# Two tiles for the block inverses, rotated queries and keys used later, and one staging buffer for raw weights, in a hybrid attention and RWKV-7 layer

## The chip, the cores and the metric

The kernel runs on one core of a Trainium2 chip, as a single launch for a whole decoder layer. The metric is the device time of one execution in microseconds, the median of several executions. Five engines work side by side, each through its own list of instructions in order: TensorE (PE, with its weight loads shown apart as PEld), VectorE (DVE), ScalarE (ACT), GpSimd (POOL) and SyncE (SP), which here does nothing but issue transfers. ACT and POOL issue transfers as well.

## The reference

One layer over 16 meta tokens and 2048 tokens of width 1024: RMSNorm, one input projection into 4640 columns, two parallel mixers, a gated merge, a residual, a SwiGLU feed-forward block and a final RMSNorm.

```python
u = rms_norm(h, norm_mix_g[layer])
proj = u @ w_in[layer] + b_in[layer]
...
q = partial_rope(q, pos)
k = partial_rope(k, pos)
y_attn = sliding_window_sink_attention(q, k, v, attn_sinks[layer])
y_rwkv = rwkv7_time_mix(p_rwkv, rwkv_mix[layer], ...)
merged = (gates[..., :D_MODEL] * (y_attn @ w_br_attn[layer])
          + gates[..., D_MODEL:] * (y_rwkv @ w_br_rwkv[layer]))
h = h + merged @ w_o[layer]
f = rms_norm(h, norm_ffn_g[layer])
h = h + (jax.nn.silu(f @ w_ffn_gate[layer]) * (f @ w_ffn_up[layer])) @ w_ffn_down[layer]
return rms_norm(h, norm_final_g)[:, N_META:]
```

The attention is a window of 128 with eight query heads, two key heads, global meta keys and a sink per head. The RWKV-7 mixer is a delta-rule recurrence with a state of 64 by 64 for each of eight heads.

## The kernel before

**Dense work.** The 2048 tokens are cut into four blocks of 512. `phase_a(b)` norms block b and makes the input projection, 37 chunks of 128 columns (one of them partly repeats). `phase_c(b)` makes the two branch products and the merge (8 chunks of `w_br`, 8 half chunks of `w_o`), then the feed-forward part (22 chunks of `w_gate`, 22 of `w_up`, 22 half chunks of `w_down`). Phase a runs for all four blocks, then phase c for all four.

**Weights.** Each product is made from three products of numbers with shortened mantissas: a weight is split into a high part (ACT copies it into a shorter type) and a low part (DVE subtracts the high part from the raw value). `chunk` does that. A weight tile `w` holds both parts of one chunk; there are three of them (tag `wsp`). The first time that a chunk is used, which is in phase a of block 0 for `w_in` and in phase c of block 0 for all the others, `chunk` takes it in two halves of 512 columns: SP loads the half into a raw tile `wraw` of 256 KB, ACT makes the high part, DVE the low part, and then POOL writes the finished pair (1 MB) to `parts_d` in HBM. For blocks 1 to 3 the finished pair is loaded whole from `parts_d`, and no raw tile is used. So 37 chunks go through the raw tiles in phase a(0) and 82 in phase c(0), with 24 products of 512 columns (a few more in phase a) on each.

**Mixers.** `attn(ti)` (tiles of 128 tokens) and `rwkv(i, j)` (256 tokens, one pair of heads) are Python generators. Each `yield` is a place where dense products are put between two of their steps. TensorE's order is fixed in exactly this program order (class `InOrder`); the order of the other engines comes from a scheduler. The dense loops yield an estimated time for each few products; for every 4 of these units each mixer in progress moves one step, the kinds in turn (`tick`). One attention tile is in progress at a time, and a new one starts when the one before it is through. Before phase c(b) starts, all mixers of blocks up to b are run to their end.

**Attention tile.** SP loads the queries `q`, a copy with swapped rows `qr`, the keys `kl` and `kr` and the values `vl`. After a `yield`, POOL rotates the queries (three instructions, L945 to L947) and the keys (`roped`, L894 to L896), ACT and DVE split the keys into `kw` (`set_keys`) and half of the queries into `qs` (`parts(0)`). Two more `yield`s later TensorE makes the scores `psS` from `qs` and `kw`. The second half of the queries is split by `parts(1)` between the two groups of heads.

**Inverses.** In each `rwkv` unit POOL solves small triangular systems (31 pairs of a product and a sum on `pr` and `xv`), writes the result to HBM (`xt_d`), and reads it back in four transfers into the diagonal blocks of `td` (L804). DVE transposes parts of `td`, TensorE and ACT fill its other corner, and the four chained steps of the unit (`ch`) read `td` as an operand up to the last of them. There is one `td` for all units; of `vd`, a like tile for the values, there are two, taken in turn.

Of the kernel before, what the change touches and what calls it, by code (L numbers as in the profile page):

```python
# [19 lines left out]
F32 = mybir.dt.float32  # L20
# [7 lines left out]
P = 128  # L28
# [50 lines left out]
def layer(ctx, tc, x, meta, w_in, w_br, w_o, w_gate, w_up, w_down, w2a, a2, g2, vecs, sinks, gfin,  # L79
# [23 lines left out]
    def late(r):  # L103

        tc.keep_in_program_order(r)
        return r
# [3 lines left out]
    cp = pool("const")  # L110
    dp = pool("dram", space=DRAM)
    dn = pool("dense")
# [5 lines left out]
    def f32(ap):  # L118
        return ap.bitcast(F32)
# [90 lines left out]
    def chunk(src, name, key, pin=False):  # L210


        w = dn.tile([P, 2, D], F32R, tag="wsp", bufs=3, name=f"w_{name}")
        if key in parts_d:
            with tc.high_priority():
                S.dma_start(f32(w.rearrange("p q c -> p (q c)")), parts_d[key])
            return w[:, 0], w[:, 1]
        for hf in range(2):
            c = slice(hf * 512, (hf + 1) * 512)
            with tc.high_priority():  # L220
                raw = dn.tile([P, 512], F32, tag="wraw", bufs=2, name=f"wr_{name}_{hf}")
                r = S.dma_start(raw, src[:, c])
                if name == "in_0_%d" % ORDER[0]:
                    late(r)
            made = HA.activation(w[:, 0, c], raw, AF.Copy), HV.tensor_sub(w[:, 1, c], raw, f32(w[:, 0, c]))
            if pin:
                late(made[0]), late(made[1])
        parts_d[key] = dp.tile([P, 2 * D], F32, name=f"wd_{name}")
        HG.dma_start(parts_d[key], f32(w.rearrange("p q c -> p (q c)")))
        return w[:, 0], w[:, 1]  # L230
# [133 lines left out]
    def phase_a(b):  # L364
        u = nxt[0] or rows_of(b)
        nxt[0] = None
        rest = None
        ws = []
        mid = lambda ci: lambda: ws.append(chunk(w_in[ci], f"in_{b}_{ci}", ("in", ci), True))
        for n_, ci in enumerate(ORDER):  # L370
            w = ws.pop(0) if ws else chunk(w_in[ci], f"in_{b}_{ci}", ("in", ci))
            if ci == ORDER[20] and b < NB - 1:
                nxt[0] = rows_of(b + 1)
            if ci == ORDER[-1] and b == NB - 1:
                nxt[0] = Ys(0)
            yield from in_chunk(b, ci, u, w, nxt[0] if ci == ORDER[-1] else None, mid(ORDER[n_ + 1]) if b == 0 and n_ < 2 else None)
            if rest:
                rest()
                rest = None
            if b == 0 and ci == ORDER[0]:  # L380
                load_rest()
                meta_norm()
            if b == 0 and ci in META_CH:
                rest = meta_chunk(ci, w)
            else:
                emitted[b].add(ci)

    def add_to_h(h, ms, src, name, key, last=None):


        ws = {}

        def part(t, hf):
            if hf not in ws:
                ws[hf] = chunk(src[hf], f"{name}_{hf}", key + (hf,))
            w = ws[hf]
            c = slice(hf * 512, (hf + 1) * 512)
            ps = psd.tile([P, 512], F32, tag="pd", name=f"ph_{name}_{t}_{hf}")
            q = slice(t * P, (t + 1) * P)
            for k in range(2):  # L400
                v = slice(k * 512, (k + 1) * 512)
                mm3(ps, ms[k][:, 0, q], ms[k][:, 1, q], w[0][:, v], w[1][:, v], k == 0, k == 1)
                yield 0.65
            HV.scalar_tensor_tensor(h[:, t, c], ps, 0.5, h[:, t, c], op0=ALU.mult, op1=ALU.add)

        if last is None:
            for hf in range(2):
                for t in range(4):
                    yield from part(t, hf)
        else:  # L410
            for t in range(4):
                for hf in range(2):
                    yield from part(t, hf)
                    last(t, hf)
# [134 lines left out]

    bkd = cp.tile([P, 2, 4, P], F32, name="bkd")  # L550
    vds = [cp.tile([P, 4, P], F32, name=f"vd{q}") for q in range(2)]
    td = cp.tile([P, 4, P], F32, name="td")
    rd = cp.tile([P, P], F32, name="rd")
    ud = cp.tile([P, P], F32, name="ud")
    for t in (bkd, *vds, td, rd):
        G.memset(t, 0.0)
    gmask = cst[:, _CC["gstrict"][0]:_CC["gincl"][1]]

# [58 lines left out]
    def rwkv(i, j):  # L617
# [3 lines left out]
        m = i is None  # L621
        uid = 4 * NU if m else 4 * i + j
# [152 lines left out]
        yield  # L775

        bt = mx.tile([P, 2, n, P], F32, tag="bt", bufs=2, name=f"bt_{nm}")
        vd = vds[(uid + m) % 2]
        for x in range(2):
            pb = psg.tile([P, 512], F32, tag="pg", name=f"pb_{nm}_{x}")  # L780
            for c in range(n):
# [98 lines left out]
    def set_keys(k, cols):  # L880
        for g in range(2):
            gb = slice(64 * g, 64 * g + 64)
            for d in (gb, slice(64 - 64 * g, 128 - 64 * g)):
                A.activation(kw[d, g, 0, cols], k[gb], AF.Copy)
                V.tensor_sub(kw[d, g, 1, cols], k[gb], f32(kw[gb, g, 0, cols]))
# [6 lines left out]
    def roped(o, src, rot, cs, w, name):  # L892

        G.tensor_mul(src, src, cs[:, 0])  # L894
        G.tensor_mul(rot, rot, cs[:, 1])
        G.tensor_add(o, src, rot)  # L896
# [28 lines left out]
    def attn(ti):  # L925
# [7 lines left out]
        q = mx.tile([P, 4, P], F32, tag="q", bufs=1, name=f"q_{ti}")  # L933
# [6 lines left out]
        load_rot(kr, 4, 1, c0, P)  # L940
        vt = mx.tile([P, P], F32, tag="vl", bufs=1, name=f"vl_{ti}")
        S.dma_start(vt, proj_d[5][:, c0:c0 + P])
        yield
        b4 = lambda k: cs[:, k].unsqueeze(1).to_broadcast([P, 4, P])
        G.tensor_mul(q, q, b4(0))  # L945
        G.tensor_mul(qr, qr, b4(1))
        G.tensor_add(q, q, qr)  # L947
        roped(kl[:, 0], kl[:, 0], kr[:, 0], cs, P, ti)
        set_keys(kl[:, 0], own)

        def parts(g):
# [75 lines left out]
    def tick():  # L1027

        turn[0] = (turn[0] + 1) % TURNS
        rs = [u for u in units if u[2] == "r"]  # L1030
        for u in list(units):
            if turn[0] != (0 if u[2] == "a" else 1 if len(rs) > 1 and u is rs[0] else 2):
                continue
            u[1] += 1
            if next(u[0], 0) == 0:
                units.remove(u)
        if todo_r and turn[0] == 2:
            i, j = todo_r[0]
            b = (i or 0) // 2
            young = min((u[1] for u in units if u[2] == "r"), default=LAG)  # L1040
            if young >= LAG - 3 and i not in asked and set(range(6, 9)) <= emitted[b]:
                asked.add(i)
                start("l", lora(i), b)
            if young >= LAG and i in loras and set(
                    range(9, 21) if i is None else range(PAIR0 + 3 * j, PAIR0 + 3 * j + 3)) <= emitted[b]:
                todo_r.pop(0)
                start("r", rwkv(i, j), b)
        if todo_a and turn[0] == 0 and not any(u[2] == "a" for u in units):
            ti = todo_a[0]
            b = (ti or 0) // 4  # L1050
            if set(range(6)) <= emitted[b]:
                todo_a.pop(0)
                start("a", attn_meta() if ti is None else attn(ti), b)
# [135 lines left out]
```

## Time and profile before

| what | us |
| --- | --- |
| median of 3 runs | 3381.07 (3380.14 to 3383.0) |
| profiled execution, own time | 3377.94 |
| its span, first to last instruction | 3376.0 |
| TensorE busy in it | 3256.3 (96%) |
| VectorE, ScalarE, GpSimd busy | 1542.1, 1163.2, 1156.1 |
| mean granted TensorE clock | 0.987 of full speed |

The profile is one execution of the kernel. Busy time of TensorE is modelled for pipelined products, so a busy TensorE isn't one at its peak. Idle time of another engine costs nothing unless TensorE waits for it in the end. Releasers of waits are inferred from semaphore events; a wait for several things is put down to the last of them. L202 is the line of a helper through which much of the dense work is recorded at high priority, so such work is told apart by its tiles.

### The profile page before, as it was taken

The page shows a single profiled execution, that of the slowest core. Times are in us where ns is not written, and L with a number is a line of the kernel's source. Part 1 is how long each engine was busy: PE and PEld are TensorE (multiplying, and loading weights), DVE is VectorE, ACT ScalarE, POOL GpSimd, SP SyncE. Part 2 cuts the span into 40 slices and gives each one's busy share as a digit, 9 for nine tenths or more (in the row PEclk, how much of TensorE's full clock was granted, in tenths as well). Part 3 has the DMA queues.
Part 4 walks back from the last instruction along what each step waited for, and adds up shares of the span by engine and source line. Part 5 has one row for each costly group of instructions (what it writes and reads, how often), then busy time and mean ns, then how long its engine had stood idle before and what let it go on. Part 6 is the DMA issues. An engine that isn't in the chain of part 4 may idle for free.

```text
span 3376.0 us, 47237 instructions
## 1 busy us (share of the span) xinstructions
PE 3256.3 (96%) x16909; PEld 2681.2 (79%) x16909; DVE 1542.1 (46%) x3622; ACT 1163.2 (34%) x2863; POOL 1156.1 (34%) x2771
## 2 busy tenths in 40 slices
PE   7899999999999998999999999999999999999998
PEld 6777887787888777887787788887888888778887
DVE  3343233232332585666666644445654443542233
ACT  4354344443443455445443422233242221220001
POOL 1124434334344454554453433444333341000000
PEclk9999999999999999999999999999999999999999
DMA  7777666676666776666668555556755555855555
GB/s 262 273 261 241 209 226 211 190 227 197 223 210 215 242 260 206 234 235 234 231 237 280 176 170 174 179 181 201 263 171 177 171 177 176 288 179 191 196 191 181
DMA packets 229448, 721.46 MB, mean 214 GB/s; under 512 B 36333, under 2 KB 90989, under 8 KB 168286
## 3 DMA queue, kind: packets, MB, share of 16 engines
q1 hardware_dynamic: 158126, 516.15, 47.1%
q0 software_dynamic: 38736, 154.99, 12.9%
q10 hardware_dynamic: 32352, 47.31, 3.8%
q8 instruction: 133, 2.18, 0.3%
q14 instruction: 101, 0.83, 0.1%
HBM read 533.46 MB, written 184.82 MB: 213 GB/s over the span
## 4 chain that ended last, share of the span: by engine, by line
PE 60%; DMA 6%; DVE 3%; POOL 3%; ACT 2%; issue 2%; SPq 0%; POOLq 0%; DVEq 0%; ACTq 0%
PE pg L93 14%; PE pu L93 12%; PE ph_d L93 11%; PE pi L93 6%; PE pb L93 4%; PE ch L93 4%; PE ph_o L93 3%; DMA yl<-y_d 1%; PE ph_o_l L93 1%; POOL pr L772 1%; POOL xv L774 1%; DMA lt<-lt_d 1%; PE py L93 1%; PE pq L93 1%; DVE h L202 1%
## 5 line engine op out<-in xcount | busy, mean ns | idle before, releaser
L93 PE MATMUL pi<-act_u,w_in 128*128 128x512 f32 x3552 | 902.5, 402 | 10.5 <-DVE m L202 6.1
L93 PEld LDWEIGHTS pi<-act_u,w_in 128*128 128x128 f32 x3552 | 652.9, 191 | 144.0 <-issue 5.5
L93 PE MATMUL pg<-act_f,w_g 128*128 128x512 f32 x2112 | 533.7, 399 | 6.8 <-DVE act_f L202 6.8
L93 PE MATMUL pu<-act_f,w_u 128*128 128x512 f32 x2112 | 522.9, 395 | 0.0
L93 PE MATMUL ph_d<-w_d,mg_g 128*128 128x512 f32 x1920 | 472.5, 397 | 10.4 <-DVE h L202 10.0
L93 PEld LDWEIGHTS pg<-act_f,w_g 128*128 128x128 f32 x2112 | 388.4, 189 | 85.3 <-DVE act_f L202 9.0
L93 PEld LDWEIGHTS pu<-act_f,w_u 128*128 128x128 f32 x2112 | 388.9, 188 | 78.8 <-issue 1.0
L93 PEld LDWEIGHTS ph_d<-w_d,mg_g 128*128 128x128 f32 x1920 | 355.5, 189 | 85.9 <-DVE h L202 14.5
L772 POOL TENSOR_TENSOR pr<-xv,lt 128x124 f32<-128x124 f32 (+30 forms) x992 | 330.5, 333 | 248.9 <-DMA lt<-lt_d 176.8
L774 POOL TENSOR_TENSOR xv<-xv,pr 128x124 f32<-128x124 f32 (+30 forms) x992 | 341.1, 344 | 74.5
L202 DVE SCALAR_TENSOR_TENSOR h<-ph_d,h 128x512 f32<-128x512 f32 x320 | 218.9, 689 | 130.0 <-PE ph_d L93 128.3
L93 PE MATMUL pb<-ya,w_br 128*128 128x512 f32 x768 | 191.0, 400 | 1.0 <-DMA w_br<-wd_br 0.6
L93 PEld LDWEIGHTS pb<-ya,w_br 128*128 128x128 f32 x768 | 143.1, 191 | 30.9 <-DVE mg_m L202 1.0
L202 DVE SCALAR_TENSOR_TENSOR th<-th,pg 128x512 f32<-128x512 f32 x88 | 60.4, 687 | 214.6 <-ACT th L202 214.5
L93 PE MATMUL ph_o<-w_o,mg_m 128*128 128x512 f32 x576 | 144.2, 400 | 6.8 <-DVE h L202 3.8
L804 POOL DMA_DIRECT2D td<-xt_d x132 | 72.6, 557 | 225.4 <-PE ch L93 197.3
L202 ACT ACTIVATE th<-pg 128x512 f32<-128x512 f32 x88 | 52.6, 598 | 281.4 <-PE pg L93 281.0
L202 DVE TENSOR_TENSOR th<-th,pu 128x512 f32<-128x512 f32 x88 | 60.5, 687 | 183.8 <-PE pu L93 183.3
L243 POOL TENSOR_TENSOR ss_o<-ss_o,mhalf 128x1 f32<-128x1 f32 x16 | 9.4, 590 | 372.5 <-DVE ss_o L202 372.3
L755 POOL DMA_DIRECT2D lt_d<-g x128 | 71.2, 561 | 184.0 <-DVE g L750 182.0
L202 ACT ACTIVATE mg_g<-th 128x512 fp32r<-128x512 f32 x88 | 55.3, 628 | 222.6 <-DVE th L202 222.5
L93 PEld LDWEIGHTS ph_o<-w_o,mg_m 128*128 128x128 f32 x576 | 106.5, 190 | 31.3 <-DVE h L202 5.2
(356 smaller groups left out, 4512.1 us busy)
## 6 DMA issues: line engine op xcount, KB each, us to landing
w_in<-wd_in SPq DMA_DIRECT2D x111, 1024.0 KB, 5.5
w_g<-wd_g SPq DMA_DIRECT2D x66, 1024.0 KB, 5.0
w_u<-wd_u SPq DMA_DIRECT2D x66, 1024.0 KB, 5.0
w_d<-wd_d SPq DMA_DIRECT2D x60, 1024.0 KB, 5.0
wd_in<-w_in POOLq DMA_DIRECT2D x37, 1024.0 KB, 5.8
w_br<-wd_br SPq DMA_DIRECT2D x24, 1024.0 KB, 7.0
wd_g<-w_g POOLq DMA_DIRECT2D x22, 1024.0 KB, 5.2
wd_u<-w_u POOLq DMA_DIRECT2D x22, 1024.0 KB, 5.3
```

Source lines behind the costliest of these rows:

```text
L93: r = f(*p, **k)
L202: return f(*p, **k)
L243: G.tensor_tensor(ss[:rows, 3:4], ss[:rows, 2:3], mhalf[:rows, 0:1], op=ALU.pow)
L755: G.dma_start(lt_d[uid, m0:m0 + n].rearrange("c j i -> j c i"), g[r32, :, 0, o])
L772: G.tensor_mul(pr[:, :, :n_], xv[:, :, r:r + 1].to_broadcast([P, 4, n_]), lt[:, r, r + 1:].unsqueeze(1).to_broadcast([P, 4, n_]))
L774: G.tensor_add(xv[:, :, r + 1:], xv[:, :, r + 1:], pr[:, :, :n_])
L804: G.dma_start(td[r32, :, r32], xt_d[uid, m0:m0 + 4].rearrange("m j i -> j m i"))
```

## The change

Three edits:

- There are two tiles `tds` instead of one `td`; a unit takes one of them by its number, as it does with `vds`.
- In `attn`, two `yield`s instead of one stand between the loads and the rotation, and two more stand between the rotation and the splitting of keys and queries into parts. A tile so has three more steps.
- The raw tile `wraw` has one buffer instead of two. (A raw tile takes 2 KB of each partition of the on-chip memory, and so does a `td`.)

```diff
@@ chunk
-                raw = dn.tile([P, 512], F32, tag="wraw", bufs=2, name=f"wr_{name}_{hf}")
+                raw = dn.tile([P, 512], F32, tag="wraw", bufs=1, name=f"wr_{name}_{hf}")
...
@@ layer
-    td = cp.tile([P, 4, P], F32, name="td")
+    tds = [cp.tile([P, 4, P], F32, name=f"td{q}") for q in range(2)]
...
-    for t in (bkd, *vds, td, rd):
+    for t in (bkd, *vds, *tds, rd):
...
@@ rwkv
-        vd = vds[(uid + m) % 2]
+        vd, td = vds[(uid + m) % 2], tds[(uid + m) % 2]
...
@@ attn
         S.dma_start(vt, proj_d[5][:, c0:c0 + P])
-        yield
+        for _ in range(2):
+            yield
         b4 = lambda k: cs[:, k].unsqueeze(1).to_broadcast([P, 4, P])
         G.tensor_mul(q, q, b4(0))
         G.tensor_mul(qr, qr, b4(1))
         G.tensor_add(q, q, qr)
         roped(kl[:, 0], kl[:, 0], kr[:, 0], cs, P, ti)
+        for _ in range(2):
+            yield
         set_keys(kl[:, 0], own)
```

## Rows read from the trace of the kernel before

**Rows 1.** The page's first part: busy time, share of the span, instructions.

```profile
PE 3256.3 (96%) x16909; PEld 2681.2 (79%) x16909; DVE 1542.1 (46%) x3622; ACT 1163.2 (34%) x2863; POOL 1156.1 (34%) x2771
```

**Rows 2.** The page's chain that ended last: shares of the span.

```profile
PE 60%; DMA 6%; DVE 3%; POOL 3%; ACT 2%; issue 2%; SPq 0%; POOLq 0%; DVEq 0%; ACTq 0%
```

**Rows 3.** Waits of TensorE, whole span: total us, times, longest us.

```profile
PE psS L93 <- DVE qs L956: 27.3, 9, 5.8
...
PE psS L93 <- ACT kw L884: 7.1, 1, 7.1
PE pq L93 <- DVE tq L808: 6.9, 2, 5.2
...
PE pb L93 <- DMA w_br<-wd_br: 0.6, 1, 0.6
```

**Rows 4.** Busy time by stretch: PE, PEld, DVE, ACT, POOL; clock, DMA share, GB/s.

```profile
40.00:280.00 240.00, 225.51 (x1172) 183.25 (x1173) 87.94 (x230) 101.86 (x226) 60.75 (x122) 0.96 0.79 276
280.00:1136.00 856.00, 831.72 (x4475) 681.03 (x4474) 274.37 (x862) 346.32 (x884) 327.66 (x817) 0.99 0.66 212
1136.00:1775.00 639.00, 610.65 (x3204) 497.54 (x3203) 429.60 (x980) 313.44 (x773) 326.85 (x707) 0.98 0.69 236
```

**Rows 5.** The raw tile of w_in from 39.57 us on: loads, and their landing.

```profile
L222 SPq DMA_DIRECT2D wr_in<-in_w_in x66: 327/332/2084, 39.6 to 274.8; - x66
...
DMA to landing us min/median/max: 2.8/4.0/7.3
```

**Rows 6.** Raw tiles in phase c(0): first and last group's instructions on ACT and DVE.

```profile
L202 ACT ACTIVATE w_br<-wr_br x16: 614/625/633, 1134.0 to 1223.8; 128x512 fp32r<-128x512 f32 x16
...
L202 DVE TENSOR_TENSOR w_d_l<-wr_d_l,w_d_l x4: 682/709/752, 1765.9 to 1772.9; 128x512 fp32r<-128x512 f32 x4
```

**Rows 7.** Timeline from 101 us, in phase a(0): start us, us, instruction.

```profile
101.37 0.63 ACT L202 ACTIVATE w_in<-wr_in 128x512 fp32r<-128x512 f32 x1
102.04 1.48 DVE L202 TENSOR_TENSOR w_in<-wr_in,w_in 128x512 fp32r<-128x512 f32 x2 [3.76 <-ACT w_in L202]
102.16 0.63 ACT L202 ACTIVATE w_in<-wr_in 128x512 fp32r<-128x512 f32 x1 [0.15 <-DMA wr_in<-in_w_in]
...
102.76 1.24 SPq L222 DMA_DIRECT2D wr_in<-in_w_in  x2
```

**Rows 8.** Waits of SP's queue, whole span: total us, times, longest us.

```profile
SPq L222 <- DVE w_in L202: 77.0, 54, 9.3
...
SPq L222 <- DVE w_u L202: 71.9, 34, 8.6
```

**Rows 9.** The raw tile of w_gate: landing of its loads.

```profile
DMA to landing us min/median/max: 2.7/3.4/9.7
```

**Rows 10.** DMA issues: count, KB each, median us to landing.

```profile
wd_g<-w_g POOLq DMA_DIRECT2D x22, 1024.0 KB, 5.2
```

**Rows 11.** Waits of POOL and ACT, whole span: total us, times, longest us.

```profile
POOL td L804 <- PE ch L93: 197.3, 25, 17.7
...
ACT qs L955 <- POOL q L947: 53.0, 13, 10.9
```

**Rows 12.** Timeline of POOL from 690 us, in phase a(2).

```profile
710.58 2.20 POOL L804 DMA_DIRECT2D td<-xt_d  x4 [17.83 <-issue]
712.80 0.47 POOL L895 TENSOR_TENSOR kr<-kr,cs 128x128 f32<-128x128 f32 x1
```

**Rows 13.** Waits of TensorE from 290 to 1147 us, phases a(1) to a(3).

```profile
PE psS L93 <- DVE qs L956: 15.0, 5, 5.8
```

**Rows 14.** Groups of TensorE from 1136 to 1775 us: busy us, mean ns, idle before.

```profile
L93 PE MATMUL py<-ptt,vz 128*128 128x512 f32 x48 | 24.6, 593 | 0.0
L93 PE MATMUL psS<-kw,qs 128*128 128x272 f32 x92 | 19.5, 337 | 8.6 <-DVE qs L956 7.6 <-ACT sig L674 0.9
```

**Rows 15.** Busy time by stretch around an idle TensorE; columns as in rows 4.

```profile
165.00:167.00 2.00, 0.18 (x1) 0.18 (x2) 0.63 (x2) 0.97 (x4) 1.08 (x2) 1.00 1.00 313
167.00:170.00 3.00, 3.00 (x8) 2.32 (x9) 0.90 (x4) 3.00 (x9) 0.55 (x1) 0.51 1.01 407
```

**Rows 16.** Timeline of TensorE: one chunk across that stretch, one before it.

```profile
119.31 5.70 PE L93 MATMUL pi<-act_u,w_in 128*128 128x512 f32 x24
...
166.82 7.34 PE L93 MATMUL pi<-act_u,w_in 128*128 128x512 f32 x24 [1.87 <-DVE m L202]
```

## The prediction

> **What bounds the kernel now.** I read the page's busy times first: TensorE is at work for 3256.3 of 3376.0 us [rows 1], so all its idle time together is 120 us. The chain that ended last says the same: 60% of it is TensorE [rows 2]. Everything that helps TensorE wait less is worth at most 120 us, while anything that starves it has no upper end. The waits of TensorE tell what little there is to win: the largest is the scores `psS` waiting for the query parts `qs`, 27.3 us in 9 waits, with 7.1 us more for the key parts `kw`. Weights hardly appear; the one wait for a weight transfer is 0.6 us [rows 3]. The reader should see there that the weight supply is now just good enough, not that it is free.
>
> So I looked at the supply by itself, in the two stretches that use the raw tiles. In phase a(0), from 40 to 280 us, TensorE is busy for 225.5 of 240 us. In phase c(0), from 1136 to 1775 us, it is busy for 610.7 of 639 us [rows 4]. From 39.6 us on, 66 halves, so 33 chunks, are loaded up to the end of phase a(0) near 280 us [rows 5]: 240/33 = 7.3 us a chunk. In phase c(0) the first conversion starts at 1134.0 us and the last ends at 1773.6 us (1772.9 plus 0.7) [rows 6]; its 82 chunks take 639/82 = 7.8 us each. TensorE sets this pace.
>
> The life of one raw tile is in the timeline. ACT starts on a half at 101.37 us, DVE follows at 102.04 us (two halves in 1.48 us, so near 0.69 each), and SP issues the next load at 102.76 us, that is 1.39 us after ACT began [rows 7]. SP's queue waits for exactly this: its load line L222 is released by DVE's `w_in` 54 times and by `w_u` 34 times [rows 8]. So a raw tile is refilled only when DVE has read it. A load takes a median of 4.0 us to land in phase a(0), 2.8 us at the least [rows 5], and for `w_gate` in phase c(0) 3.4 and 2.7 us [rows 9]. With two raw tiles, two such cycles run side by side, which gives a chunk in 4.0 + 1.39 = 5.4 us, under the 7.3 that TensorE needs.
>
> **The raw tile, one instead of two.** Now the second half of a chunk can't start to load before DVE has finished with the first. A chunk costs two cycles in a row: load, land, ACT, DVE, load, land, ACT, DVE. The three weight tiles let the loader run ahead, but a buffer evens out a pace, it doesn't raise it. The cycle's terms:
>
> - Landing. The rows show 2.7 to 4.0 us, the latter with two raw loads in flight together. With one in flight there is less beside it, but the 1 MB write-back of the pair (5.2 us) [rows 10] remains, and starts just when the next half is issued. I take 3.3 us as an estimate between the two, nearer to `w_gate`'s median.
> - Conversion: 1.39 us [rows 7].
> - Delay in the queues of ACT, DVE and SP. An instruction in progress there lasts some 0.7 us, so a conversion that becomes ready meets on average half of one, times the busy share. In phase a(0), DVE is busy 37% (87.9 of 240) and ACT 42%: 0.13 + 0.15, near 0.3 us. In phase c(0), DVE is busy 67% (429.6 of 639) and ACT 49% [rows 4]: 0.24 + 0.17 = 0.4. Each is served in order and also stands waiting for TensorE's mixer products, and SP carries the mixers' loads in the same queue; I double it to 0.8 us.
>
> Phase a(0): 3.3 + 1.39 + 0.3 = 5.0 us a half, times 66 = 329 us against 240: +89. Phase c(0): 3.3 + 1.39 + 0.8 = 5.5 us a half, times 164 = 902 us against 639: +263. Together +352 us. Blocks 1 to 3 load finished pairs and pay nothing.
>
> Bounds from the rows. From below: shortest landing, no delay. Phase a(0) 2.8 + 1.39 = 4.2, times 66 = 277 (+37); phase c(0) 2.7 + 1.39 = 4.1, times 164 = 672 (+33): +70 us. From above: a landing of 4.0 in both and delays of 0.4 and 1.4: 5.8 times 66 = 383 (+143), 6.8 times 164 = 1115 (+476): +619 us. Nothing of it can hide: the cover for a slow loader would be TensorE's own work, and that is what the 240 and 639 us already are.
>
> **Two tiles for the inverses.** POOL waits 197.3 us in all at L804, where the reload of `td` must let the former unit's `ch` products finish [rows 11]. One such wait of 17.8 us ends at 710.58 us, and the rotation of a tile's keys stands right behind it at 712.80 us [rows 12]. With a second tile the wait is for the unit before the last and should be gone; memory clearing at the start adds one instruction. What does TensorE gain? POOL isn't the bound. What is late next on this path is the inverse itself: TensorE waited 6.9 us for its transposed copy `tq` [rows 3], and that comes out of the solving, not out of the wait. So directly at most those 6.9 us; the rest acts through the rotation.
>
> **The attention steps.** No instruction is added: the same loads, three rotations of queries and three of keys on POOL, the same splits on ACT and DVE. They move by one step (rotation) and three steps (splits) against the dense products. ACT stood 53.0 us for POOL's rotated `q` before `qs` [rows 11], and TensorE 27.3 + 7.1 us behind that [rows 3]. The moved rotation and the earlier POOL should end nearly all of these. But what falls into phases a(0) and c(0) will be covered by the starved loader anyway. What is worth something is the stretch from 290 to 1147 us: 15.0 us [rows 13]. I take -15 us for both edits together; from 0 (POOL's order brings other waits) to -25 (`tq` and the time of a lower clock after each idle stretch as well).
>
> A tile now has 20 steps instead of 17, so 80 estimated units instead of 68. By the program's own counts (770 units for the four phases a, 430 for a phase c, a first tile near 74) about 10.2 tiles lay in phase a, 5.8 in c(0) and none in c(1); now it is 8.7, 5.4 and 1.9. So 0.4 tile leaves the covered stretch. Its large products take 24.6/6 us for the values (eight a tile, 48 in all) and 19.5 x 16/92 us for the scores [rows 14], some 7.5 us, so 3 us for 0.4 of it: left out.
>
> **Sum.** 3377.9 (the profiled execution's own time) + 352 - 15 = 3715 us. That execution was 3.1 us under the median of the runs, which is a tenth of a per cent and far below the terms' uncertainty: I forecast 3715.
>
> **Rivals.** First, *the landing falls to its floor*. With one raw load in flight, each might land in 2.7 or 2.8 us and meet free engines: +70 - 15, so about 3435 us. For it: the shortest landings are there in both stretches [rows 5, 9]. Against it: the medians are 0.7 to 1.2 us above, with a write-back beside most loads. The Trainium skill ("DMA: Bandwidth & Descriptors", section on the anatomy of one DMA) gives about 2.0 us fixed plus bytes over 436 GB/s for a transfer issued by GpSimd; as an estimate from that page a lone 256 KB load takes 2.6 us and the sum would be some 30 us lower still. The shortest landings agree with it; these loads are SP's, and their medians do not.
>
> Second, *the clock falls as well*. The trace shows TensorE idle for 1.87 us before 166.82 us, and the granted clock at 1.00 in the stretch before 167 us and at 0.51 (its lower level, 1.2 GHz) in the 3 us after it [rows 15]; the chunk across it took 7.34 us, where one before took 5.70 us [rows 16]. A starved TensorE will idle like this in most chunks. At the lower level its work per chunk, 610.7/82 = 7.4 us in c(0) and 225.5/33 = 6.8 us in a(0) [rows 4], would double to 14.9 and 13.7, over the loader's 11.0 and 10.0. But then TensorE doesn't idle, and the clock comes back. Half-way between, 12.9 and 11.8 us, costs 82 x 1.9 + 33 x 1.8 = 215 us more: 3930 us. For it: the idle gaps will recur. Against it: as long as TensorE stays under the loader's pace a low clock costs nothing. The Trainium skill ("TensorE: Matmul & The Clock Gate", section on HAM oscillation) tells of a kernel whose wait for each slice of weights dropped the clock anew every time; by that rule this rival gains weight, and the low clock after the 1.87 us above agrees with it.
>
> Third, on the other side, *not slower*. If the loader keeps ahead, the waits for `qs` and `kw` go (34 us, to about 3340 us). It is decided at one place: a half's cycle must stay under 3.65 us in phase a(0) and 3.9 us in c(0) (half of 7.3 and 7.8), so a landing under 2.3 and 2.5 us. No load in the rows lands that fast. Last, *the change does nothing that shows*: the scheduler might keep the loader out of TensorE's way and the POOL wait might just move; 3380 us. Against it speaks the same cycle.
>
> **How the numbers follow.** The loader's pace as worked out: 0.77, with a range of its own of 3570 to 3840 us (landings of 3.0 and 3.6, delays of 0.1 to 0.3 and 0.5 to 1.1, gains of 25 and 5). The floor 0.10, the low clock 0.08, not slower 0.03, nothing 0.02. To leave out no more than 2 in 10, the range runs from 3500 to 3890: it leaves out the floor, the two cases at or below the present time, and about half of the low clock's. A difference under 0.2% can't be told from none here. Faster: 0.03; the same: 0.02; slower: 0.77 + 0.10 + 0.08 = 0.95.
>
> **What would show it.** In the profile after: phases a(0) and c(0) longer by about 90 and 260 us, TensorE's busy share there down to 65 to 75%, and TensorE's list of waits led by the conversions (DVE or ACT writing `w_in`, `w_g`, `w_u`, `w_d`). The loads of one chunk follow each other at 5 us or more instead of 0.6 us. The wait of POOL at L804 is gone, the waits of `psS` are small, and the phases of blocks 1 to 3 take the time they took, less some 15 us. I am wrong if the loads of both halves still overlap, if landings stay under 2.5 us, or if the blocks after the first change by more than the loader does.

## The result and the profile after

The changed kernel takes 3625.28 us (3619.71 to 3635.32) against 3380.61 us: 1.0736 times the time, 95% interval 1.0712 to 1.0760. The forecast was 3715 us within 3500 to 3890. The direction, the mechanism and the stage that pays are as forecast; the size of the loss is 245 us instead of 337.

The profiled execution took 3621.15 us. The page's busy times and its chain that ended last:

```profile
PE 3355.6 (93%) x16909; PEld 2694.4 (74%) x16909; DVE 1540.0 (43%) x3622; ACT 1171.0 (32%) x2863; POOL 1141.2 (32%) x2772
...
PE 64%; DMA 20%; DVE 6%; ACT 5%; POOL 3%; issue 2%; SPq 0%; ACTq 0%; POOLq 0%; DVEq 0%
PE pi L93 16%; PE pg L93 12%; PE pu L93 10%; PE ph_d L93 9%; DMA wr_in<-in_w_in 6%; PE pb L93 4%; PE ch L93 4%; DMA wr_g<-in_w_gate 3%; DMA wr_u<-in_w_up 3%; PE ph_o L93 2%; DMA wr_d<-in_w_down 2%; PE py L93 1%; ACT w_in L202 1%; DVE w_in L202 1%; DMA wr_o<-in_w_o 1%
```

Transfers hold 20% of the chain, where they held 6% [rows 2], and the raw weights `wr_in`, `wr_g`, `wr_u` and `wr_d` are named in it. TensorE has the same 16909 instructions, yet 99 us more busy time than before [rows 1]. The mean granted clock is 0.972 instead of 0.987, which explains some 57 us of it (0.028 of 3619 us less 0.013 of 3376); the rest is not accounted for.

Where the time went shows when TensorE ends its last dense product of each phase (read from the timeline, in us; each figure is the length of the phase):

| phase | before | after | difference |
| --- | --- | --- | --- |
| a(0), with 16 to 18 us of start | 296.6 | 385.2 | +88.6 |
| a(1), a(2), a(3) | 288.6, 290.5, 274.5 | 274.5, 274.2, 271.2 | -33.7 |
| c(0) | 641.3 | 823.1 | +181.8 |
| c(1) | 568.3 | 582.4 | +14.1 |
| c(2), c(3) | 545.9, 461.3 | 541.9, 457.5 | -7.8 |

Two phases pay 270 us, the others give back 27. In the view by stretches the two are cut by the loader's own ends (us; busy us of PE, PEld, DVE, ACT, POOL; clock, DMA share, GB/s), the counterpart of [rows 4]:

```profile
41.20:380.60 339.40, 267.37 (x1211) 187.95 (x1209) 89.08 (x230) 105.07 (x230) 63.81 (x129) 0.95 0.60 210
380.60:1189.50 808.90, 799.42 (x4350) 657.77 (x4350) 255.48 (x803) 323.37 (x820) 312.43 (x798) 1.00 0.67 217
1189.50:2015.20 825.70, 689.18 (x3229) 522.20 (x3229) 438.07 (x986) 325.56 (x781) 322.56 (x720) 0.91 0.55 189
2015.20:3618.60 1603.40, 1574.95 (x7994) 1307.25 (x7994) 739.65 (x1559) 393.56 (x985) 432.98 (x1098) 0.99 0.58 194
```

TensorE is busy for 79% and 83% of the loader's two stretches, and the DMA engines work less there than before, 0.60 and 0.55 instead of 0.79 and 0.69: nobody is at a limit, everybody waits in turn. The timeline of phase a(0) shows the turn (start us, us, instruction); it answers to [rows 7]:

```profile
69.59 5.19 SPq L222 DMA_DIRECT2D wr_in<-in_w_in  x2
73.07 0.63 ACT L202 ACTIVATE w_in<-wr_in 128x512 fp32r<-128x512 f32 x1 [2.32 <-DMA wr_in<-in_w_in]
73.73 0.69 DVE L202 TENSOR_TENSOR w_in<-wr_in,w_in 128x512 fp32r<-128x512 f32 x1 [3.29 <-ACT w_in L202]
77.42 0.63 ACT L202 ACTIVATE w_in<-wr_in 128x512 fp32r<-128x512 f32 x1 [3.14 <-DMA wr_in<-in_w_in]
78.08 0.69 DVE L202 TENSOR_TENSOR w_in<-wr_in,w_in 128x512 fp32r<-128x512 f32 x1 [3.32 <-ACT w_in L202]
78.80 0.33 SPq L222 DMA_DIRECT2D wr_in<-in_w_in  x1
```

The first row holds two loads, at 69.59 us and just after DVE's end at 74.42 us; the third comes at 78.80 us. That is one half every 4.6 us, where two were issued within 1.3 us before [rows 7]. The raw tiles of `w_in` from 41.2 us on, and below the second "..." those of `w_gate`, landed so, against 4.0 and 3.4 us [rows 5, 9]:

```profile
L222 SPq DMA_DIRECT2D wr_in<-in_w_in x68: 327/328/521, 41.2 to 374.4; - x68
...
DMA to landing us min/median/max: 2.6/3.1/8.4
...
DMA to landing us min/median/max: 2.6/3.1/7.0
```

68 halves in 339.4 us make 5.0 us a half; 164 in 825.7 us of phase c(0) make 5.0 as well. TensorE's list of waits has changed hands (total us, times, longest us):

```profile
PE pi L93 <- ACT w_in L202: 64.2, 48, 5.9
PE ph_d L93 <- ACT w_d L202: 38.3, 19, 4.6
PE pg L93 <- ACT w_g L202: 25.3, 16, 4.5
PE pu L93 <- ACT w_u L202: 15.4, 16, 2.7
PE ph_o L93 <- ACT w_o L202: 11.6, 4, 3.7
```

The query parts, first in [rows 3], are gone from it. POOL's reload of `td` waits for `ch` 5 times and 18.4 us instead of 25 and 197.3 [rows 11]; what comes last now is the inverse's own way through HBM:

```profile
POOL td L804 <- DMA xt_d<-xv: 55.9, 17, 5.5
POOL td L804 <- PE ch L93: 18.4, 5, 4.6
```

### The profile page after: what moved, and what is told of

The parts are those of the page before. It is cut to its first block, busy times and chain, and to the rows that moved or that the text cites. A ratio compares the mean times of both kernels' runs of the same rounds, so it can differ in the third digit from the quotient of the medians.

```text
span 3618.6 us, 47223 instructions
## 1 busy us (share of the span) xinstructions
PE 3355.6 (93%) x16909; PEld 2694.4 (74%) x16909; DVE 1540.0 (43%) x3622; ACT 1171.0 (32%) x2863; POOL 1141.2 (32%) x2772
## 3 DMA queue, kind: packets, MB, share of 16 engines
q0 software_dynamic: 38736, 154.99, 11.7%
## 4 chain that ended last, share of the span: by engine, by line
PE 64%; DMA 20%; DVE 6%; ACT 5%; POOL 3%; issue 2%; SPq 0%; ACTq 0%; POOLq 0%; DVEq 0%
PE pi L93 16%; PE pg L93 12%; PE pu L93 10%; PE ph_d L93 9%; DMA wr_in<-in_w_in 6%; PE pb L93 4%; PE ch L93 4%; DMA wr_g<-in_w_gate 3%; DMA wr_u<-in_w_up 3%; PE ph_o L93 2%; DMA wr_d<-in_w_down 2%; PE py L93 1%; ACT w_in L202 1%; DVE w_in L202 1%; DMA wr_o<-in_w_o 1%
## 5 line engine op out<-in xcount | busy, mean ns | idle before, releaser
L93 PE MATMUL pi<-act_u,w_in 128*128 128x512 f32 x3552 | 928.1, 407 | 75.5 <-ACT w_in L202 64.2
L93 PE MATMUL pg<-act_f,w_g 128*128 128x512 f32 x2112 | 546.3, 403 | 36.2 <-ACT w_g L202 25.3
L93 PE MATMUL pu<-act_f,w_u 128*128 128x512 f32 x2112 | 534.6, 400 | 18.7 <-ACT w_u L202 15.4
L93 PE MATMUL ph_d<-w_d,mg_g 128*128 128x512 f32 x1920 | 498.6, 409 | 44.5 <-ACT w_d L202 38.3
L93 PEld LDWEIGHTS ph_d<-w_d,mg_g 128*128 128x128 f32 x1920 | 363.7, 195 | 136.8 <-ACT w_d L202 47.7
L861 POOL TENSOR_TENSOR gst<-gst,mhalf 128x4 f32<-128x4 f32 x32 | 33.5, 1046 | 450.6 <-DVE gst L860 445.9
L93 PE MATMUL ph_o<-w_o,mg_m 128*128 128x512 f32 x576 | 153.7, 416 | 17.4 <-ACT w_o L202 11.6
L202 DVE TENSOR_TENSOR w_in<-wr_in,w_in 128x512 fp32r<-128x512 f32 x74 | 53.2, 719 | 201.5 <-ACT w_in L202 201.5
```

The costliest lines, as they stand in the source:

```text
L93: r = f(*p, **k)
L202: return f(*p, **k)
L861: G.tensor_tensor(st[:, 3], st[:, 2], mhalf[:, 0:4], op=ALU.pow)
```

## The experiments

The theory: with one raw tile, load and conversion of each half stand one behind the other, and the chunk's pace is the number of pieces, divided by the number of raw tiles, times one cycle of landing, conversion and delays. Rivals: the moved steps or the second `td` make part of the loss; the bytes, or the number of transfers in SP's queue, set the pace. Phase lengths are read from one execution of each kernel. Each time stands beside the kernel before, run on the same chip.

**One raw tile alone.** The kernel before, with

```diff
-                raw = dn.tile([P, 512], F32, tag="wraw", bufs=2, name=f"wr_{name}_{hf}")
+                raw = dn.tile([P, 512], F32, tag="wraw", bufs=1, name=f"wr_{name}_{hf}")
```

> The kernel before with one raw tile and nothing else changed. Theory: the loader alone makes the loss; phases a(0) and c(0) grow by about 90 and 185 us as they do after the whole change, and the 27 us that the other stages gained are not there: about 3650 us. Rival: a part of the loss comes from the moved attention steps or from the second td (TensorE's order, SP's queue): 3480 to 3600 us.

Measured: 3657.57 us, ratio 1.0827 (1.0803 to 1.0851). Phase a(0) grows by 97.6 us, c(0) by 195.9; the six other phases together are 11.7 us shorter, so that a part of the 27 us was there without the other two edits. Its waits of TensorE show both troubles side by side, the new one and the old one:

```profile
PE pi L93 <- ACT w_in L202: 70.5, 47, 5.7
PE ph_d L93 <- ACT w_d L202: 44.2, 20, 3.7
PE psS L93 <- DVE qs L956: 15.2, 5, 5.0
```

The raw tile by itself costs more than the whole change, so the rival falls. The other two edits gain.

**Two raw tiles with the rest of the change.** Two raw tiles beside two `td` make four tiles of 2 KB, where the kernels before and after have three. Room for the fourth comes from the transposed weights of the attention, which take the place of `qr`; that tile is done with by then:

```diff
-                raw = dn.tile([P, 512], F32, tag="wraw", bufs=1, name=f"wr_{name}_{hf}")
+                raw = dn.tile([P, 512], F32, tag="wraw", bufs=2, name=f"wr_{name}_{hf}")
...
-                pt = mx.tile([P, 512], F32, tag="pt", bufs=1, name=f"ptt_{nm}_{o}")
+                pt = mx.tile([P, 4, P], F32, tag="qr", bufs=1, name=f"ptt_{nm}_{o}").rearrange("p j t -> p (j t)")
```

> The changed kernel with two raw tiles again; room for them is made by letting the tile ptt of the transposed weights share the place of qr. Theory: phases a(0) and c(0) are back at 280 and 640 us or a little less, the gains in the other stages stay, and the waits of psS for qs go: 3335 to 3360 us. Rival: the second td and the moved steps gain nothing by themselves: 3375 to 3390 us.

Measured: 3353.25 us, ratio 0.9932 (0.9909 to 0.9955): 0.7% faster than the kernel before. Phases a(0) and c(0) take 276.2 (after the start) and 627.6 us, where before had 280.3 and 641.3. Its loads of `w_gate` land in a median of 3.6 us again:

```profile
DMA to landing us min/median/max: 2.6/3.6/10.3
```

**One raw tile of 256 columns**, in the changed kernel (`range(4)`, `c = slice(hf * 256, (hf + 1) * 256)`, a tile of `[P, 256]`, one buffer):

> The changed kernel with one raw tile of 256 columns: four cycles in a row for each chunk. Theory (each load pays a landing that depends little on its size): 4 x 3.85 = 15.4 us a chunk against 10.1, over 33 + 82 chunks about 610 us more: 4150 to 4300 us. Rival (the rate of the bytes sets the pace, and smaller pieces move as many): 3600 to 3700 us.

Measured: 4167.0 us, ratio 1.2340 (1.2315 to 1.2365). The same bytes, in pieces half as large, cost 540 us more than the whole change did. The rival that the bytes set the pace falls. In the trace a cycle is 3.7 us, four in a row 14.7 us a chunk. Landing in phase a(0) and for `w_gate`:

```profile
DMA to landing us min/median/max: 2.2/2.3/10.6
...
DMA to landing us min/median/max: 2.2/2.3/6.2
```

Half the bytes saved only 0.8 us of 3.1, and each chunk now pays the remaining 2.3 us four times instead of 3.1 twice.

**Two raw tiles of 256 columns**, the same with `bufs=2`, so the memory of the change's one tile:

> The changed kernel with two raw tiles of 256 columns, so the same memory as its one of 512, and four loads a chunk. Theory (what costs is that nothing is in flight while a raw tile is converted): two cycles of about 2.9 + 0.1 + 0.85 us side by side give a chunk in 7.7 us, near TensorE's own pace: 3345 to 3420 us. Rival (the bytes in flight or their number on SP's queue decide): 3600 us or more.

Measured: 3542.5 us, ratio 1.0492 (1.0472 to 1.0512): a miss for the theory's number, and for the rival's. A second small tile, and so overlap, took 625 us off the time with one, and the result is 83 us under the change itself, in the same memory. The number of loads is the same with one small tile and with two, so that number alone doesn't set the pace. But I had put the cycle at 3.85 us from medians. Each load's issue, landing, start of ACT and end of DVE in the trace give a mean landing of 3.25 us in phase a(0) and 3.05 in c(0), a conversion of 0.96 and 1.19, delays of 0.27 and 0.45: 4.5 and 4.7 us, two of them 9.0 and 9.4 a chunk, and 9.1 and 9.5 were measured. (These parts fill the interval from one load of a tile to the next, so that they add up is no test of the theory; the forecast time was the test.) The slow landings belong in the sum: the median for `w_gate` is only 2.5 us, the longest 6.6.

```profile
DMA to landing us min/median/max: 2.2/2.5/6.6
```

**Four raw tiles of 128 columns**, the same with `range(8)`, 128 columns, `bufs=4`:

> The changed kernel with four raw tiles of 128 columns, again in the memory of its one of 512. Two tiles of 256 gave a cycle of 4.5 to 4.7 us (mean landing 3.05 to 3.25, conversion 0.96 to 1.19, delays 0.3 to 0.5), two cycles a chunk. Theory (overlap counts): a landing of about 2.9, a conversion of 0.8 and delays of 0.5 make 4.2 us, again eight loads over four tiles, so 8.4 us a chunk against 9.3: about 3440 us (3390 to 3500). Rival (each piece costs time in the queues of SP, ACT and DVE, which more and smaller pieces make worse): 3540 us or more.

Measured: 3583.89 us, ratio 1.0618 (1.0593 to 1.0643): the expectation of 3440 missed, the rival's bound held. The mean landing didn't fall below that of the pieces twice as large (3.26 and 3.05 us), and the delays grew to 0.83 and 0.82 us, more than half of it in phase a(0) before SP issues the next load. The cycle is 4.8 and 4.9 us, a chunk 9.6 and 9.85. So the theory needs its second half: overlap sets the divisor, but going from two pieces in flight to four half as large didn't shorten the cycle.

```profile
L222 SPq DMA_DIRECT2D wr_in<-in_w_in x296: 327/382/1657, 2.7 to 359.8; - x148
...
DMA to landing us min/median/max: 1.8/2.8/10.0
```

**The moved steps alone**, in the kernel before:

```diff
         S.dma_start(vt, proj_d[5][:, c0:c0 + P])
-        yield
+        for _ in range(2):
+            yield
...
         roped(kl[:, 0], kl[:, 0], kr[:, 0], cs, P, ti)
+        for _ in range(2):
+            yield
         set_keys(kl[:, 0], own)
```

> The kernel before with the moved attention steps alone: one td, two raw tiles. Theory (the steps end the waits of psS and nearly all of the gain is theirs): phases a(1) and a(2) shorter by about 14 us each, total 3350 to 3362 us, about 0.993 of before. Rival (POOL's wait for td held the rotation up and the second td is what helps): 3370 to 3382 us.

Measured: 3353.63 us, ratio 0.9943 (0.9927 to 0.9959). Phases a(1) to a(3) are 32.5 us shorter, c(0) 6.8, c(1) 18.9 longer. POOL still waits for the one `td`, even longer than before, and it doesn't matter (total us, times, longest us):

```profile
POOL td L804 <- PE ch L93: 227.1, 29, 19.4
```

In phases a(1) to a(3) TensorE's wait for `qs`, 15.0 us [rows 13], is gone; what is left of `psS` there is one wait of 0.6 us for another engine. The rival, that POOL's wait held the rotation up, is not needed for this gain.

**The changed kernel without the second `td`, and without the moved steps.** Each with one raw tile of 512 columns:

> The changed kernel without the second td: one raw tile, moved steps. Theory (the gain is the steps'): 3620 to 3632 us, as the changed kernel. Rival (the gain is the second td's): 3645 to 3660 us, as with one raw tile alone.

> The changed kernel without the moved steps: one raw tile, two td. Theory: 3645 to 3660 us, as one raw tile alone, with POOL's wait at the reload of td gone and TensorE no better off. Rival: 3620 to 3635 us.

Measured: 3633.18 us, ratio 1.0766 (1.0745 to 1.0788), and 3635.04 us, ratio 1.0770 (1.0751 to 1.0789), against 1.0827 for one raw tile alone and 1.0736 for the whole change. The first is 1 us above the theory's range and 12 us under the rival's. The second misses the theory and lies at the rival's upper end: the second `td` by itself is worth some 0.5% there, the steps by themselves 0.6%, and the two together 0.9%, which at these intervals can't be told from the sum of the two. TensorE did gain by the second `td`, against what I expected: its wait for `qs` is 7.6 us instead of 15.2, and its wait for `tq` in c(1) to c(3) is gone from the list (first line with the second `td`, last line with one raw tile alone):

```profile
PE psS L93 <- DVE qs L956: 7.6, 3, 3.5
...
PE pq L93 <- DVE tq L808: 4.1, 2, 2.3
```

By phases the second `td` gains 6.6 us in c(1) to c(3), where no attention and no raw tile is left, and 17.7 us in a(0) and c(0); a(1) to a(3) lose 3.9. The 12.0 us in a(0) can hardly be `td`'s own work: with one raw tile alone its first reload is at 346.3 us, and most of the gain is there before it (the 65th half is converted at 341.3 us, with the second `td` at 333.4). The mean landing there is 3.63 us with one raw tile alone and 3.51 with the second `td` as well. Whether the other order of SP's and POOL's transfers does that, or chance in one execution, wasn't settled. The second `td` alone beside two raw tiles was not run.

## Why the prediction was right, and where its sizes were off

**The raw tile** was the right term, and the serial cycle the right mechanism: loads 4.6 us apart in the timeline, the list of waits led by the conversions, the DMA engines less busy, and 283 us of loss with that edit alone. In phase a(0) the sum was 5.0 us a half and +89 us; measured were 5.0 and +87 (without the start). In phase c(0) it was 5.5 us and +263; measured were 5.0 and +182. The forecast loss was 337 us and the measured one 245: 81 of the 92 us between them are in that one term, the rest in the gains of the other edits. Its landing was taken as 3.3 us; the median is 3.1 and the mean over all loads 3.35, so that was right. The conversion was right. What failed is the doubled delay of 0.8 us for queues in phase c(0): by the trace, waits before ACT (0.2 us), between ACT and DVE (0.1) and before the next issue (0.05) come to some 0.35 us there. The doubling is the larger part of the error; no row stood behind it, and the 0.4 us before it was near. The smaller part is that I had taken the busy shares of DVE and ACT from the kernel before. When TensorE starves, their work spreads over 826 us instead of 639, and DVE's share falls from 67% to 53%, ACT's from 49% to 39%; by these shares the undoubled sum gives 0.3 us. That the starved TensorE lets the converting engines answer sooner is argued from these shares and was not tested by itself.

**The floor** as a rival: single loads got down to 2.6 us, but their mean didn't, so it didn't come about. **The low clock** did come, and cost nothing that shows: the granted clock was 0.91 in c(0), so about a sixth of that stretch stood at the lower level, and 0.95 in a(0). The pace stayed at two loader cycles a chunk all the same, as the rival's counter-argument had it: the engines that convert waited for loads and for each other, and hardly for TensorE. For `w_gate` the trace gives what ended their idle time (us, times):

```profile
  DMA wr_g<-in_w_gate: 107.0, 39
  ACT w_g L202: 67.7, 34
  PE ch L93: 0.3, 1
```

The low clock shows in the busy time instead: at a mean of 0.91 instead of 0.98 the same products take some 60 us longer in c(0) (0.09 of 826 us less 0.02 of 639), of the 79 us by which TensorE's busy time there grew. That is some 7 points of the busy share of 83% there, where I had forecast 65 to 75%; another 6 come from the stretch being 826 us long and not 902. In a(0) the share was 79%, and the clock explains little of it: over the whole phase it was 0.95 instead of 0.97, some 10 of the 32 us by which TensorE's busy time grew. The rest stays open. The Trainium skill ("TensorE: Matmul & The Clock Gate", section on HAM oscillation) describes such a drop in a kernel that waits for the next slice of an operand. This trace agrees: with the waits for weights the mean clock in c(0) fell from 0.98 to 0.91. It also shows the drop hidden behind a slower loader.

**The second `td` and the steps** were put at -15 us together. The phases without a raw tile gave 27 us. I had also said that what falls into a(0) and c(0) would be covered by the starved loader. It was not all covered: beside one raw tile alone, the whole change takes 10.3 us less in a(0) (without the start) and 14.1 in c(0). The mechanism of the steps was right: the waits for `qs` went, also with one `td` (steps alone). The tiles moved as counted: 32 products `psS` are made after 2015 us, two tiles' worth where 1.9 were forecast.

```profile
L93 PE MATMUL psS<-kw,qs 128*128 128x272 f32 x32 | 6.7, 336 | 0.0
```

That is why a(1) to a(3) gain 33.7 us and c(1) loses 14.1: some 16 us of TensorE's work only changed place (the groups of attention products come to 98 us before and 82 after in the stretch from the end of the raw `w_in` to the first `w_br`). For the second `td` I held at most 6.9 us possible; c(1) to c(3) gained 6.6 in the experiment, with the wait for `tq` 4.1 us less, though I had said that this wait comes out of the solving alone. But the whole came to some 0.5% with one raw tile. With two raw tiles, both edits (0.9932) and the steps alone (0.9943) can't be told apart, so a gain of the second `td` isn't shown there.

## What to carry to other kernels

A staging buffer's pace is pieces, divided by buffers in flight, times the whole cycle of landing, conversion and reissue; put that beside what the consumer takes for a chunk before giving a buffer away, however deep the queue of finished tiles behind it is. Sum with mean landings, not medians; don't double a delay without a row that calls for it, and take the busy shares of the helping engines from the time that the new pace will give them. Even so the cycle of smaller pieces came out 0.6 to 0.9 us longer than I had summed it, so it has to be measured. When memory has to be found, share the place of tiles whose lives don't meet, rather than cut the one buffer that hides a latency: here that was the difference between a loss of 7.4% and a gain of 0.7%.

## What the hardware showed that was not expected

A load's landing fell much less than its size: a median of 3.1 us for 256 KB and 2.3 us for 128 KB with one in flight, and no less (2.8 us) for 64 KB with four in flight. Cutting the same memory into four smaller tiles was slower (3584 us) than into two (3543 us). And TensorE's busy time rose by 99 us for the very same instructions, a little over half of it by the lower clock, so busy time alone says little of a starved TensorE; its waits and the granted clock have to be read with it.
